# An FFN output product done as a two-by-two block product with seven block matmuls

## The chip, the cores and the metric

The kernel runs on one core of one Trainium2 chip. The metric is the device time of one launch in microseconds; the time before is the median of three runs. A profiled execution of the same program gives the trace that the rows below come from.

## The reference, cut to what matters

One encoder layer on 1024 tokens of width 1024. It begins and ends with a half-step feed-forward network (FFN) of 2816 features, and the change concerns both of these:

```
def _swiglu(x, w_in, w_out):
    gate, up = jnp.split(x @ w_in, 2, axis=-1)
    return (jax.nn.silu(gate) * up) @ w_out

x = x + 0.5 * _swiglu(_rmsnorm(x, n1_g), ffn1_w_in, ffn1_w_out)
...                                # projections, two attention mixers, merge
x = x + 0.5 * _swiglu(_rmsnorm(x, n3_g), ffn2_w_in, ffn2_w_out)
return _rmsnorm(x, nf_g)
```

With g = silu(gate) * up, the product that is changed is g @ w_out: 1024 tokens by 2816 features by 1024 outputs.

## The kernel before

**Number format.** Every operand of a large product is split by `split` (L81) into two fp32r numbers: ScalarE (ACT) casts it to `hi` (L82), VectorE (DVE) subtracts to get `lo` (L83). A product is then three matmuls, hi by hi, hi by lo and lo by hi.

**First half of an FFN, `ffn_in` (L321).** It walks the 22 feature tiles (128 features each). The product with `w_in` is already a two-by-two block product with seven block matmuls per tile: seven weight operands are made by `ffn_weights` (L297, additions on GpSimd, called POOL, at L309; splits on ACT and DVE), and the seven token operands are fixed (`operands`, L228: four of them live in the big buffers `bigA` and `bigB`, three in a pool `ex`). `product` (L335) issues 12 matmuls of 128x512 per operand into three PSUM banks, some of which it continues after a copy was taken (the copies are L354, L357, L360, L363). The result g of a tile is split, and stored to a DRAM buffer `g_d` as `goh`/`gol` halves (two stores of 512 KB for a tile); the last two tiles are kept in SBUF.

**Second half, `ffn` (L381).** x (4 MB) is loaded once and stays in SBUF. `out_rows` (L215) takes two feature tiles at a time: for each of 8 token tiles and 2 output halves it issues 6 matmuls of 128x512 (`mm3`, L118) into one of three PSUM banks tagged `S`, and DVE adds the bank to x (L226). The two tiles kept come first, then pairs whose g halves are loaded from `g_d` (four loads of 512 KB, contiguous 4 KB per partition) and whose weights (`weights`, L88) come from `w_out` as two rows blocks of 512 KB, split in 1024-wide instructions. The last tiles (two in the first FFN, four in the second) are handed back as a function and run interleaved with the norm that follows. In the second FFN, two of these last tiles lie in a buffer `spare` in `bigA`.

**Order.** The program is written in the order above, but a list scheduler orders the instructions of each engine before the run: an instruction written earlier goes first among those that are ready in its own timing model, and loads go out as soon as their buffer is free there. All DMAs go through one queue on SyncE (SP). On the chip every engine takes its list strictly in order.

```
# L215, the loop of out_rows
for t in tiles:
    for n in range(2):
        po = self.bank("S")
        ...
        self.mm3(po, [...])                    # 6 matmuls for a pair of feature tiles
        nc.vector.scalar_tensor_tensor(xs, po, scale, xs, ALU.mult, ALU.add)
```

Of the kernel before, what the change touches and what calls it, by code (L numbers as in the profile page):

```python
# [19 lines left out]
P = 128  # L20
SEQ = 1024
# [18 lines left out]
FILL_LATER = 250  # L40
EDGE = 280


class Layer:
# [276 lines left out]
    def ffn_in(self, w_in, ops, ph, g_d, first, ws):  # L321
# [16 lines left out]
        for i in range(NF):  # L338
# [7 lines left out]
            gh, gl = (ph.tile([P, SEQ], F32R, tag="t4", name=self.uid("g"), bufs=self.t4) for _ in range(2))  # L346
            for c in range(0, 512, m):
                cols = slice(c, c + m)
                w = iter(ws)
                bx, by, bz = (self.bank(t)[:, :m] for t in ("mm", "tp", "S"))  # L350
                e1, e2, e3, e5 = (ph.tile([P, 512], F32, tag="t2", name=self.uid("e"), bufs=8)[:, :m]
                                  for _ in range(4))
                product(bx, next(w), ops["b11"], cols, True)
                nc.scalar.copy(e1, bx)  # L354
                product(by, next(w), ops["b21"], cols, True)
                product(bx, next(w), ops["t2"], cols, False)
                nc.scalar.copy(e2, bx)  # L357
                nc.vector.tensor_tensor(e1, by, e1, ALU.add)
                product(bz, next(w), ops["t1"], cols, True)
                nc.scalar.copy(e5, bz)  # L360
                nc.scalar.activation(e1, e1, AF.Silu)
                product(bx, next(w), ops["t3"], cols, False)
                nc.scalar.copy(e3, bx)  # L363
                nc.gpsimd.tensor_tensor(e3, e3, e5, ALU.add)
                product(bz, next(w), ops["b22"], cols, False)
                nc.vector.tensor_tensor(e2, bz, e2, ALU.add)
                nc.scalar.activation(e2, e2, AF.Silu)
                nc.vector.tensor_tensor(e2, e2, e3, ALU.mult)
                product(bx, next(w), ops["t4"], cols, False)
                nc.vector.tensor_tensor(e1, bx, e1, ALU.mult)  # L370
                for n, e in ((1, e2), (0, e1)):
                    tok = slice(n * 512 + c, n * 512 + c + m)
                    self.split(gh[:, tok], gl[:, tok], e)
            if i < NF - 2:
                self.dma(g_d[i, 0], gh)
                self.dma(g_d[i, 1], gl)
            else:
                kept.append((gh, gl))
        return kept

    def ffn(self, x_d, w_in, w_out, g_d, ex, es_ex, first, ws=None, big=False):  # L381


        ph, es_ph = self.open("ph", bufs=1)
        ops = ex if first is None else self.operands(ex)
        self.t4 = 4 if first is None else 6
        kept = self.ffn_in(w_in, ops, ph, g_d, first, ws)
# [6 lines left out]
        def load(pool, f):  # L394
            out = []
            for i in (f, f + 1):
                g = [pool.tile([P, SEQ], F32R, tag=t, name=self.uid(t), bufs=2) for t in ("goh", "gol")]
                for j in range(2):
                    self.dma(g[j], g_d[i, j])
                out.append(tuple(g))  # L400
            return out
# [4 lines left out]
        self.w_eng = self.nc.vector  # L406
        self.out_rows(x, kept, weights(NF - 2), 0.5, range(NT))
        es_ph.close()
        go, es_go = self.open("go", bufs=1)
        end = 4 if big else 2  # L410
        for n, f in enumerate(range(0, NF - 4, 2)):
            cur = load((xo, go)[n % 2], f), weights(f)
            if f < NF - 2 - end:
                self.out_rows(x, *cur, 0.5, range(NT))
        f = NF - 4
        if big:
            spare = self.hp.tile([P, 8, SEQ], F32R, tag="bigA", name=self.uid("spare"))
            g, w = [(spare[:, 2 * j], spare[:, 2 * j + 1]) for j in range(2)], []
            for j in range(2):
                for h in range(2):  # L420
                    self.dma(g[j][h], g_d[f + j, h])
                raw = self.raw()
                self.dma(raw, w_out[(f + j) * P:(f + j + 1) * P, :])
                w.append((spare[:, 4 + 2 * j], spare[:, 5 + 2 * j]))
                self.split(*w[j], raw)
            cur = cur[0] + g, cur[1] + w
        else:
            cur = load(go, f), weights(f)

        def close():  # L430
            es_go.close()
            es_xo.close()

        return x, lambda tiles: self.out_rows(x, *cur, 0.5, tiles), close
# [494 lines left out]
    def run(self):  # L929
# [11 lines left out]
        g_d = [self.dr.tile([NF - 2, 2, P, SEQ], F32R, name=f"g_d{j}") for j in range(2)]  # L941
# [4 lines left out]
        def first(ops, ph):  # L946
            xs = {}

            def load(ts):
                for t in ts:  # L950
                    xs[t] = ph.tile([P, D], F32, tag="t4", name=self.uid("x0"), bufs=6)
                    self.dma(xs[t], x_d[t])
# [20 lines left out]
        x, rows, close = self.ffn(x_d, io["ffn1_w_in"], io["ffn1_w_out"], g_d[0], ex, es_ex, first)  # L973
# [94 lines left out]
        x, rows, close = self.ffn(x2_d, io["ffn2_w_in"], io["ffn2_w_out"], g_d[1], ops2, es_ex, None, ws, True)  # L1068
# [56 lines left out]
```

## Time and profile before

| | us |
|---|---|
| median of 3 runs | 2391.39 (2390.85 to 2392.74) |
| profiled execution, its own time | 2389.99 |
| span of its trace | 2388.2 |
| mean granted TensorE clock | 0.978 |

The span runs from the first to the last instruction of the trace; the execution's own time has 1.8 us more around it. PE is TensorE's matmuls, PEld its weight loads, DVE VectorE, ACT ScalarE, POOL GpSimd, SP the queue that issues all DMAs. Matmul ends in the trace are modelled: successive matmuls overlap, so the distance between starts, not the duration, is what one costs.

### The profile page before, as it was taken

The numbers are of one execution on the slowest core, as the hardware profiler recorded it, in microseconds if no ns is written. First come the engines' busy times: TensorE is split into PE (matmuls) and PEld (weight loads), VectorE is DVE, ScalarE is ACT, GpSimd is POOL, SyncE is SP. The second block draws the span as 40 slices with busy tenths as digits, with TensorE's granted clock in tenths as the row PEclk, the third lists the DMA queues.
The fourth block names the chain that finished last, engine by engine and source line by source line (L and its number), as shares of the span: only waits on it lengthen the run. The fifth ranks groups of instructions, "written<-read, shape, count | busy, mean of one in ns | idle before, by whom it ended". The sixth has DMA issues, their size and how long they took to land. (4 is left out here: it accounts for less than half of the span.)

```text
span 2388.2 us, 30574 instructions
## 1 busy us (share of the span) xinstructions
PE 2265.6 (95%) x10928; PEld 1893.1 (79%) x10928; DVE 1517.9 (64%) x2917; ACT 1010.3 (42%) x1971; POOL 589.8 (25%) x492
## 2 busy tenths in 40 slices
PE   4999999999998999899998999999799999999998
PEld 3877777778887988687778888878688888878886
DVE  7555555456657459798895378677655555546565
ACT  5444444410104454667743377633444444431012
POOL 6433333100005000223220043221733343300000
PEclk7999999999999999899999999999799999999999
DMA  4233333354414023455523241373233333354331
GB/s 134 89 106 106 106 106 106 106 203 159 159 71 146 1 80 98 131 127 136 126 71 103 87 159 49 112 250 110 89 106 115 106 106 106 106 218 169 132 142 71
DMA packets 204217, 280.82 MB, mean 118 GB/s; under 512 B 12064, under 2 KB 150304, under 8 KB 203552
## 3 DMA queue, kind: packets, MB, share of 16 engines
q1 hardware_dynamic: 204064, 278.86, 35.9%
q8 instruction: 86, 1.41, 0.3%
q14 instruction: 67, 0.55, 0.1%
HBM read 186.55 MB, written 79.69 MB: 111 GB/s over the span
## 5 line engine op out<-in xcount | busy, mean ns | idle before, releaser
L226 DVE SCALAR_TENSOR_TENSOR x<-S,x 128x512 f32<-128x512 f32 x400 | 270.6, 689 | 201.6 <-PE S L118 200.8
L83 DVE TENSOR_TENSOR wop<-raw,wop 128x512 fp32r<-128x512 f32 x210 | 150.3, 723 | 204.5 <-ACT wop L82 203.9
L82 ACT CAST whi<-raw 128x1024 fp32r<-128x1024 f32 (+1 forms) x90 | 85.6, 974 | 413.9 <-PE S L118 335.8
L335 PE MATMUL mm<-bigA,wop 128*128 128x512 f32 (+1 forms) x736 | 236.4, 384 | 10.6 <-ACT e L357 10.6
L335 PE MATMUL S<-bigA,wop 128*128 128x512 f32 (+1 forms) x736 | 235.1, 382 | 5.3 <-POOL wop L83 4.1
L118 PE MATMUL S<-wlo,goh 128*128 128x512 f32 x608 | 236.8, 389 | 0.0
L118 PE MATMUL S<-whi,gol 128*128 128x512 f32 x608 | 236.7, 389 | 0.0
L118 PE MATMUL S<-whi,goh 128*128 128x512 f32 x608 | 232.9, 393 | 1.9 <-DVE bigB L83 1.5
L82 ACT CAST wop<-raw 128x512 fp32r<-128x512 f32 x224 | 137.4, 625 | 103.7 <-PE mm L335 44.9
L335 PEld LDWEIGHTS mm<-bigA,wop 128*128 128x128 f32 x736 | 136.6, 188 | 46.0 <-ACT e L357 19.8
L118 PE MATMUL mm<-bigA,whi 128*128 128x512 f32 x384 | 156.0, 406 | 16.0 <-ACT whi L82 10.0
L83 DVE TENSOR_TENSOR wop<-s,wop 128x512 fp32r<-128x512 f32 x84 | 91.5, 1090 | 115.7 <-ACT wop L82 115.4
L335 PEld LDWEIGHTS S<-bigA,wop 128*128 128x128 f32 x736 | 137.6, 190 | 32.7 <-POOL wop L83 4.5
L118 PE MATMUL mm<-bigA,wlo 128*128 128x512 f32 x384 | 155.2, 405 | 2.1 <-POOL wlo L83 2.1
L118 PE MATMUL mm<-bigB,whi 128*128 128x512 f32 x384 | 154.9, 403 | 0.2 <-DVE bigB L83 0.2
L643 POOL TENSOR_SCALAR p<-p,z 128x640 f32<-128x640 f32 (+7 forms) x128 | 92.5, 726 | 211.8 <-DVE z L642 143.9
L83 POOL TENSOR_TENSOR wlo<-raw,whi 128x1024 fp32r<-128x1024 f32 (+1 forms) x32 | 67.7, 2114 | 301.1 <-ACT whi L82 292.3
L335 PE MATMUL S<-bigB,wop 128*128 128x512 f32 (+1 forms) x368 | 140.4, 382 | 0.1
L335 PE MATMUL mm<-bigB,wop 128*128 128x512 f32 (+1 forms) x368 | 139.8, 380 | 0.0
L118 PEld LDWEIGHTS S<-whi,goh 128*128 128x128 f32 x608 | 114.1, 188 | 31.5 <-DVE x L226 6.3
L309 POOL TENSOR_TENSOR raw<-raw,s 128x512 f32<-128x512 f32 x42 | 54.6, 1300 | 332.4 <-DVE wop L83 332.4
L335 PE MATMUL mm<-b,wop 128*128 128x512 f32 (+1 forms) x552 | 134.5, 381 | 0.0
(257 smaller groups left out, 5375.4 us busy)
## 6 DMA issues: line engine op xcount, KB each, us to landing
raw<-in_ffn_w_in_dram SPq DMA_DIRECT2D x88, 512.0 KB, 4.1
g_d<-g SPq DMA_DIRECT2D x80, 512.0 KB, 5.0
raw<-in_ffn_w_out_dram SPq DMA_DIRECT2D x44, 512.0 KB, 6.9
goh<-g_d SPq DMA_DIRECT2D x38, 512.0 KB, 5.2
gol<-g_d SPq DMA_DIRECT2D x38, 512.0 KB, 6.1
raw<-in_w_in_dram SPq DMA_DIRECT2D x28, 512.0 KB, 5.4
x<-in_x_dram SPq DMA_DIRECT2D x16, 512.0 KB, 7.5
x_d<-x SPq DMA_DIRECT2D x16, 512.0 KB, 2.6
```

What stands on the lines that cost most here:

```text
L82: self.nc.scalar.copy(hi, src)
L83: (eng or self.nc.vector).tensor_tensor(lo, src, hi.bitcast(F32), ALU.subtract)
L118: nc.tensor.matmul(out, lhsT=a, rhs=b, start=(i == 0), stop=(i == len(steps) - 1))
L226: nc.vector.scalar_tensor_tensor(xs, po, scale, xs, ALU.mult, ALU.add)
L309: nc.gpsimd.tensor_tensor(out, x, y, op)
L335: nc.tensor.matmul(out, lhsT=l, rhs=r, start=start and j == 0, stop=j == len(steps) - 1, skip_group_check=True)
L643: nc.gpsimd.tensor_scalar(p, p, z, 1.0, ALU.mult, ALU.mult)
```

## The change

For 16 of the 22 feature tiles (`NS = 16`), the output product is done in eight pairs of tiles. For a pair, the token rows p and p+4 and the two feature tiles make a two-by-two block matrix of g, the two feature tiles and the two output halves one of w_out, and the block product is formed from seven block products in place of eight.

- In `ffn_in`, the seven g operands of a pair are made as soon as both tiles of g are there: four 128x512 additions on POOL, seven splits, and seven stores of 512 KB to a new DRAM buffer `gs_d` (before: four splits and four stores of 512 KB for a pair). One operand is made after the even tile, six after the odd one. The temporary tag `t2` gets 10 buffers in place of 8; the tag `t4` has 4 buffers in both FFNs (before 6 in the first). Two of the first x tiles use the tag `s`.
- In `ffn`, `weight_ops` makes the seven weight operands of a pair: four 128x512 subtractions on POOL and seven 512-wide splits, into one of three 32 KB slots (`bigA`, `bigB`, and one in the pool `go`).
- `load_parts` loads the operands of a pair for one token pair p: 14 runs of 512 B per partition, 896 KB. Two pairs are worked at a time; the operands of the next p are loaded into the other of two pools while the current block runs.
- `block_rows` issues 42 matmuls for two pairs and one p: seven block products of 6 matmuls into three banks. Bank bx takes products 0, 2, 4 and 6, each continuing the sum in it; bz takes 3 and 5; by takes 1. After each product DVE adds the bank to a part of x, and the next product into this bank follows that addition.
- The four remaining streamed tiles (16 to 19) are loaded into the third slot as eight loads of 512 KB (`rest`); the two tiles kept are done first, as before, with `out_rows`.

```diff
+NS = 16
 def ffn_in(...)
-            if i < NF - 2:
-                self.dma(g_d[i, 0], gh)
-                self.dma(g_d[i, 1], gl)
...
+            def part(q, j, src):
+                t = ph.tile([P, SEQ], F32R, tag="t4", bufs=4).rearrange("p (h c) -> p h c", h=2)
+                self.split(t[:, 0], t[:, 1], src)
+                self.dma(gs_d[q, :, 2 * j:2 * j + 2, :], t)
...
+            elif i % 2 == 0:
+                a11, a21 = e1, e2
+                part(q, 0, a11)
             else:
+                a12, a22 = e1, e2
+                s1 = ph.tile([P, 512], F32, tag="t2", bufs=10)
+                nc.gpsimd.tensor_tensor(s1, a21, a22, ALU.add)
+                part(q, 1, a12)
+                nc.gpsimd.tensor_tensor(a21, a11, a21, ALU.subtract)
+                part(q, 6, a22)
+                nc.gpsimd.tensor_tensor(a11, s1, a11, ALU.subtract)
+                part(q, 3, s1)
+                nc.gpsimd.tensor_tensor(a12, a12, a11, ALU.subtract)
+                part(q, 4, a21)
+                part(q, 2, a11)
+                part(q, 5, a12)
 def ffn(...)
+        slots = [self.hp.tile([P, 8, 2, 512], F32R, tag=t) for t in ("bigA", "bigB")]
+        def weight_ops(q):
+            ra, rb, rs = self.raw(), self.raw(), self.raw()
+            for r, f in ((ra, 2 * q), (rb, 2 * q + 1)):
+                self.dma(r, w_out[f * P:(f + 1) * P, :])
+            b11, b12, b21, b22, t3, t2 = (r[:, c:c + h] for r in (ra, rb, rs) for c in (0, h))
+            sub(t3, b22, b12)
+            sub(b12, b12, b11)
+            sub(t2, b22, b12)
+            dst = slots[q % 3]
+            for j, src in enumerate((b11, b21, t2, b12, t3, b22, b21)):
+                self.split(dst[:, j, 0], dst[:, j, 1], src, self.w_eng)
+                if j == 1:
+                    sub(b21, b21, t2)
+            return dst
+        def load_parts(q, p):
+            t = pools[p % 2].tile([P, 7, 2, P], F32R, tag="gs", bufs=2)
+            self.dma(t.rearrange("p o h c -> p (o h) c"), gs_d[q, :, :, p * P:(p + 1) * P])
+            return t
+        def block_rows(ws, gs, p):
+            bx, by, bz = (self.bank(t) for t in ("mm", "tp", "S"))
+            done = {0: ((p, 0),), 1: ((p, 0),), 2: ((p, 1),), 3: ((p + 4, 1),),
+                    4: ((p + 4, 1),), 5: ((p, 1),), 6: ((p + 4, 0),)}
+            for j, bank in enumerate((bx, by, bx, bz, bx, bz, bx)):
+                ...                       # 6 matmuls, start only for j in (0, 1, 3)
+                for t, n in done[j]:
+                    add(t, n, bank)
+        for c in range(0, NS // 2, 2):
+            nxt = []
+            for p in range(4):
+                ahead = None
+                if p < 3:
+                    ahead = [load_parts(c + k, p + 1) for k in range(2)]
+                elif c + 2 < NS // 2:
+                    ahead = [load_parts(c + 2 + k, 0) for k in range(2)]
+                if p == 0 and c + 2 < NS // 2:
+                    nxt.append(weight_ops(c + 2))
+                block_rows(ws, gs, p)
+                gs = ahead
+            if nxt:
+                nxt.append(weight_ops(c + 3))
+                ws = nxt
+        rest = slots[2]...                # the third slot, seen as 4 tiles x 2 halves x 1024
+        for f in range(4):
+            for j in range(2):
+                self.dma(rest[:, f, j], g_d[f, j])
```

## Rows read from the trace of the kernel before

**Rows 1.** The page: busy time by engine, and TensorE's granted clock in 40 slices.

```profile
PE 2265.6 (95%) x10928; PEld 1893.1 (79%) x10928; DVE 1517.9 (64%) x2917; ACT 1010.3 (42%) x1971; POOL 589.8 (25%) x492
PEclk7999999999999999899999999999799999999999
```

**Rows 2.** The chain of waits near its start: start us, us, what.

```profile
2141.52 0.70 DVE x L226
2142.22 0.04 issue
2142.27 234.40 PE S L118 x1026
```

**Rows 3.** Busy time by stretch, with granted clock, DMA share and GB/s.

```profile
2142.00:2376.00 234.00, 233.73 (x1024) 191.67 (x1025) 140.68 (x219) 29.39 (x39) 0.00 (x0) 1.00 0.37 138
500.00:732.00 232.00, 229.83 (x1009) 187.50 (x1008) 140.38 (x212) 27.90 (x37) 10.50 (x6) 1.00 0.36 135
2127.00:2142.00 15.00, 13.25 (x56) 9.96 (x54) 7.68 (x9) 6.38 (x9) 1.30 (x1) 1.00 0.98 383
1695.00:1705.00 10.00, 5.45 (x22) 4.79 (x23) 6.18 (x6) 2.38 (x5) 10.00 (x8) 0.50 0.00 1
```

**Rows 4.** Groups by line and operation: xcount, busy us, mean ns, idle before.

```profile
L226 DVE SCALAR_TENSOR_TENSOR x<-S,x 128x512 f32<-128x512 f32 x400 | 270.6, 689 | 201.6 <-PE S L118 200.8 <-DMA sgm<-bra_d 0.7
L82 ACT CAST wop<-raw 128x512 fp32r<-128x512 f32 x224 | 137.4, 625 | 103.7 <-PE mm L335 44.9 <-PE S L335 33.1 <-PE tp L335 11.7
L309 POOL TENSOR_TENSOR s<-raw 128x512 f32<-128x512 f32 x42 | 54.7, 1304 | 27.8 <-DVE wop L83 22.6 <-DMA raw<-in_ffn_w_in_dram 5.2
L309 POOL TENSOR_TENSOR raw<-raw,raw 128x512 f32<-128x512 f32 x48 | 80.4, 1677 | 0.0
```

**Rows 5.** The timeline of DVE where one pair of tiles follows another.

```profile
2160.30 0.69 DVE L226 SCALAR_TENSOR_TENSOR x<-S,x 128x512 f32<-128x512 f32 x1 [0.67 <-PE S L118]
2160.90 2.35 DVE L83 TENSOR_TENSOR wlo<-raw,whi 128x1024 fp32r<-128x1024 f32 x2
2163.47 1.89 DVE L226 SCALAR_TENSOR_TENSOR x<-S,x 128x512 f32<-128x512 f32 x3 [0.21 <-PE S L118]
```

**Rows 6.** The timeline of POOL and DVE in the first half of the second FFN.

```profile
1870.36 1.29 POOL L364 TENSOR_TENSOR e<-e,e 128x512 f32<-128x512 f32 x1 [6.00 <-ACT e L363]
1872.27 1.30 POOL L309 TENSOR_TENSOR s<-raw 128x512 f32<-128x512 f32 x1 [0.62 <-DVE wop L83]
...
1870.83 1.36 DVE L83 TENSOR_TENSOR wop<-s,wop 128x512 fp32r<-128x512 f32 x1 [2.47 <-ACT wop L82]
1872.41 0.69 DVE L366 TENSOR_TENSOR e<-S,e 128x512 f32<-128x512 f32 x1 [0.22 <-PE S L335]
```

**Rows 7.** Write regions: first product of the first FFN, a later write into its operand.

```profile
36.92 0.58 PE L335 MATMUL S<-bigA,wop 128*128 128x256 f32 x1
59.78 0.58 ACT L82 CAST bigA<-tp 128x512 fp32r<-128x512 f32 x1
```

**Rows 8.** The timeline of SP's queue around the start of the second FFN's output.

```profile
2139.54 4.11 SPq L79 DMA_DIRECT2D spare<-g_d  x4
2144.66 0.33 SPq L79 DMA_DIRECT2D raw<-in_ffn_w_out_dram  x1
2160.33 0.32 SPq L79 DMA_DIRECT2D goh<-g_d  x1
```

**Rows 9.** DMA from 1886.2 to 1890 us: one w_in load, 512 B runs, alone.

```profile
DMA packets 1041, 0.54 MB, mean 142 GB/s; under 512 B 16, under 2 KB 1040, under 8 KB 1040
q1 hardware_dynamic: 1040, 0.52, 47.1%
DMA to landing us min/median/max: 3.6/3.6/3.6
```

**Rows 10.** DMA from 600 to 660 us: loads with 4 KB runs alone.

```profile
q1 hardware_dynamic: 2592, 9.44, 42.1%
```

**Rows 11.** The w_in loads of 1850 to 1960 us, stores of g beside them.

```profile
DMA to landing us min/median/max: 3.6/4.7/5.3
```

**Rows 12.** Waits of PE in the first half of each FFN (80 to 480, 1740 to 2130 us): total us, times, longest.

```profile
PE mm L335 <- ACT e L357: 8.5, 19, 0.5
PE mm L335 <- ACT e L354: 0.8, 1, 0.8
...
PE mm L335 <- ACT e L357: 1.4, 2, 0.7
```

**Rows 13.** Waits of PE from 1685 to 1714 us.

```profile
PE S L335 <- POOL wop L83: 4.1, 1, 4.1
```

More of the change, by code (lines that the diff above doesn't have):

```diff
@@ L319, in ffn_weights, with feature, ffn_in @@
             yield w
-    def ffn_in(self, w_in, ops, ph, g_d, first, ws):
+    def feature(self, w, ops, cols, product, e1, e2, e3, e5):
+        nc = self.nc
+        m = e1.shape[1]
+        bx, by, bz = (self.bank(t)[:, :m] for t in ("mm", "tp", "S"))
+        product(bx, next(w), ops["b11"], cols, True)
+        nc.scalar.copy(e1, bx)
+        product(by, next(w), ops["b21"], cols, True)
+        product(bx, next(w), ops["t2"], cols, False)
+        nc.scalar.copy(e2, bx)
+        nc.vector.tensor_tensor(e1, by, e1, ALU.add)
+        product(bz, next(w), ops["t1"], cols, True)
+        nc.scalar.copy(e5, bz)
+        nc.scalar.activation(e1, e1, AF.Silu)
+        product(bx, next(w), ops["t3"], cols, False)
+        nc.scalar.copy(e3, bx)
+        nc.gpsimd.tensor_tensor(e3, e3, e5, ALU.add)
+        product(bz, next(w), ops["b22"], cols, False)
+        nc.vector.tensor_tensor(e2, bz, e2, ALU.add)
+        nc.scalar.activation(e2, e2, AF.Silu)
+        nc.vector.tensor_tensor(e2, e2, e3, ALU.mult)
+        product(bx, next(w), ops["t4"], cols, False)
+        nc.vector.tensor_tensor(e1, bx, e1, ALU.mult)
+    def ffn_in(self, w_in, ops, ph, g_d, gs_d, first, ws):
         nc = self.nc
@@ L345, in ffn_in @@
                 ws = first(ops, ph)
-            gh, gl = (ph.tile([P, SEQ], F32R, tag="t4", name=self.uid("g"), bufs=self.t4) for _ in range(2))
+            e1, e2, e3, e5 = (ph.tile([P, 512], F32, tag="t2", name=self.uid("e"), bufs=10) for _ in range(4))
             for c in range(0, 512, m):
[L348 to L370, printed above, removed]
@@ L392, in ffn @@
             self.dma(x[:, t, :], x_d[t])
[L394 to L401, printed above, removed]
+        self.w_eng = nc.vector
+        slots = [self.hp.tile([P, 8, 2, 512], F32R, tag=t, name=self.uid("slot")) for t in ("bigA", "bigB")]
@@ L403, in weights @@
         def weights(f):
             return [self.weights((w_out[i * P:(i + 1) * P, :], D)) for i in (f, f + 1)]
-        self.w_eng = self.nc.vector
-        self.out_rows(x, kept, weights(NF - 2), 0.5, range(NT))
+        w = weights(NF - 2)
+        ws = [weight_ops(q) for q in (0, 1)]
+        gs = [load_parts(q, 0) for q in (0, 1)]
+        self.out_rows(x, kept, w, 0.5, range(NT))
         es_ph.close()
         go, es_go = self.open("go", bufs=1)
[L410 to L414, printed above, removed]
@@ L415, in ffn @@
-        f = NF - 4
-        if big:
[L417 to L421, printed above, removed]
+        slots.append(go.tile([P, 8, 2, 512], F32R, tag="slot", name=self.uid("slot")))
+        gsp, es_gsp = self.open("gsp", bufs=1)
+        pools.append(gsp)
+        for c in range(0, NS // 2, 2):
[13 more added lines that the diff above has]
+                ws = nxt
@@ L423, in ffn @@
                 self.dma(raw, w_out[(f + j) * P:(f + j + 1) * P, :])
[L424 removed]
+                w.append(tuple(last.tile([P, D], F32R, tag=f"w{j}{k}", name=self.uid("w")) for k in range(2))
+                         if j == 3 else tuple(self.wp.tile([P, D], F32R, tag=k, name=self.uid(k), bufs=3)
+                                              for k in ("whi", "wlo")))
                 self.split(*w[j], raw)
[L426 removed]
@@ L427, in ffn @@
         else:
-            cur = load(go, f), weights(f)
+            es_last = None
+            self.out_rows(x, g[:2], weights(f), 0.5, range(NT))
+            g, w = g[2:], weights(f + 2)
         def close():
+            if es_last is not None:
+                es_last.close()
             es_go.close()
             es_xo.close()
-        return x, lambda tiles: self.out_rows(x, *cur, 0.5, tiles), close
+        return x, lambda tiles: self.out_rows(x, g, w, 0.5, tiles), close
     def rope(self, y, t, nh, pool):
```

55 lines of the change are left out of this document (46 added, 9 removed).

## The prediction, on record before the changed kernel ran

> **What bounds the kernel now.** I read the page first: TensorE works in 95% of the span and no other engine in more than 64% [rows 1]. Then the chain of waits: from 2142.27 us to the end of the second FFN's output it is one piece, 1026 matmuls in 234.40 us, with no wait of note in it [rows 2]. That is 0.2285 us for one matmul of 128x512, the unit of all that follows. Third the stretches: in both output stages PE is busy all the time at a granted clock of 1.00, VectorE for 60% and the DMA engines for 0.36 to 0.37 [rows 3]. So a matmul less here is time less, as long as VectorE, the loads and the weights keep up. The question is how much of the room beside PE the change uses up.
>
> **What it removes.** A pair of feature tiles costs 2 x 8 x 2 x 3 = 96 matmuls now and 4 x 7 x 3 = 84 afterwards. Eight pairs and two FFNs: 192 matmuls less, 192 x 0.2285 = 43.9 us. The rest of the sum is what is lost of this. A block of `block_rows` is 42 matmuls, 9.60 us, and there are 16 in an FFN; one of its seven products is 1.37 us.
>
> **Load of the token operands (d).** A block needs two loads of 896 KB, 3584 runs of 512 B, while the block before it runs, since their buffers come free when the block before that ends. The nearest row is a load of w_in with the same run length, alone on the queue: 1040 packets at 47.1% of 16 engines over 3.8 us, 27.5 ns for each packet, and 3.6 us from issue to landing, so 1.8 us of fixed delay around 1.8 us of data [rows 9]. Two loads: 3584 x 27.5 / 16 = 6.2 us of data + 1.8 + 0.3 for the issue = 8.3 us, against 9.60: hidden, with 1.3 us to spare. Weights for the next pairs share the queue. A 512 KB load with 4 KB runs takes 128 x 175 / 16 = 1.4 us (2592 packets, 42.1% of 60 us, [rows 10]); two that stand ahead of the token loads cost 2.8 - 1.3 = 1.5 us. I take one such meeting per FFN, 3 us; below nothing if they fall into the gaps, and above, if the landing scales whole with the packets from the median of 4.7 us that loads beside stores show [rows 11], 4.7 x 3.5 = 16.4 us a block, 6.8 us too many 30 times.
>
> The Trainium skill's page "DMA: Bandwidth & Descriptors" (Specifications) gives 512 B as the size from which a transfer runs at line rate. By that the two loads would take 1.835 MB at the 383 GB/s that long runs reach [rows 3], 4.8 us, and d would be nothing. The trace does not bear it out: 512 B in 27.5 ns is 18.6 GB/s an engine, 4 KB in 175 ns is 23.4.
>
> **VectorE and the weights in the blocks (a).** Additions hardly change in number (7 in place of 8 for the same 48 matmuls' work), 0.69 us each [rows 4]. Splits do: seven of 512 columns for a pair in place of two of 1024 (1.18 us each, [rows 5]). In four blocks, 38.4 us, VectorE has 28 x 0.69 = 19.3 us of additions and 14 x 0.69 = 9.7 us of splits. ACT (14 x 0.625 = 8.8 us) and POOL (8 subtractions of 1.3 to 1.7, at most 13.4 us) stay well below 38.4 [rows 4], so they cost nothing while PE covers them.
>
> What is new is that an addition now holds PE up sooner. Before, three banks let it be late: at 2160.90 two splits of 2.35 us went ahead, three additions piled up behind them, and the stage did not stop [rows 5]. Now product 2 writes into the bank that the addition after product 0 reads, with 1.37 us between. The modelled end lies 0.16 us behind the slot, the addition takes 0.70 and PE follows about 0.05 after [rows 2], so it may be late by 0.4 us, and by one product more where PE's list puts an independent product (3, in another bank) ahead. Splits come first again, being written earlier. First block: the third slot opens when the kept tiles are done, and seven splits are ready together, 4.8 us; 4.8 - 0.4 - 1.4 = 3.0 us lost. At the two later places where a slot opens, subtractions on POOL spread the splits; I take a third of it, 1 us each. The other slot is refilled piece by piece during the block that uses it last: buffers are tracked by region, since PE read one half of a `bigA` operand at 36.92 us and ACT still wrote the other at 59.78 [rows 7]. That costs nothing that I can see. Sum 5 us an FFN, **a = 10**. Bounds: 2 us if the lists interleave well, 36 if VectorE itself limits (a rival).
>
> **Passing from the first half to the second (b).** The first two pairs' splits, 14 x 0.69 = 9.7 us, fall on the two kept tiles (96 matmuls, 21.9 us, with 16 x 0.69 = 11.0 us of additions): 20.7 of 21.9 us. Nine splits can come in one go, 6.2 us, while three banks hold 4.1. I take 1.5 us an FFN, **b = 3**; from 0 to 12.
>
> **The four remaining tiles (c).** Their eight loads go into the third slot, whose last reader is the third group's last block, and a load leaves as soon as its buffer is free: four loads into `spare` left at 2139.54, 180 us ahead of their use [rows 8]. So six or eight of them, 8.2 to 10.9 us at 1.4 each, stand before the next token loads. These are then late: data from 15.7 us (7.5, where the load before ends, + 8.2), landing near 22.4 where 19.2 is wanted, a loss of 3.2 us; 5.9 with all eight in front, 8.7 with two weights as well. I take 5 us an FFN, **c = 10**, from 4 to 17. Waits up to 0.8 us left the clock at 1.00 in these stages [rows 3, 12]. After waits of up to 4.1 us it was at 0.50, the lower of its levels, 1.2 of 2.4 GHz, in the stretch of 1695 to 1705 [rows 3, 13]. Such a stretch could add 5 us (10 us of matmuls at half the rate) to each of two stalls; I take none and keep 10 for the range.
>
> **The first half (e).** It gets three splits and three stores more for a pair, and four operations on POOL. In the 38 us of a pair that is 3 x 0.69 on VectorE, 3 x 0.625 on ACT, 4 x 1.3 to 1.7 on POOL [rows 4] and 3 x 1.4 us of DMA [rows 10]: all behind PE. On SP a store that waits for its split holds up the w_in loads behind it, which are wanted a tile later, 19 us. The copies out of PSUM on ACT are not all hidden: in the first FFN PE waits for them 19 times, 8.5 us, in the second only twice, 1.4 us [rows 12], in the same code. More work on ACT, unevenly placed (one operand after an even tile, six after an odd one), can bring this order into the second FFN (+8.5), and a new order can lose it in the first (-8.5). I take half of the first, **e = 4**, from -8 to 17. Without the cover, all casts and splits of the part show: 3 x (0.69 + 0.625) x 8 = 32 us an FFN. The moved x tiles and the buffer counts I cost at nothing: the loads still leave in the same order, and `t4` had 4 buffers in the second FFN already.
>
> **Sum.** -43.9 + 10 + 3 + 10 + 3 + 4 = -13.9 us. Against the profiled execution, 2390.0 (span 2388.2 and 1.8 around it), that is 2376.1; the median of the runs is 1.4 above it: **2377.5 us**. Changes under 0.2%, 4.8 us, can't be told from none.
>
> **Rivals.**
>
> *Loads longer than a block (slower).* Place: each of 30 blocks; price: 30 x (load - 9.60). Without d, 16.9 us of gain are left, and 21.7 must be lost to count as slower, so it decides from 0.72 us over, a load of 10.3 us. For it: loads beside stores landed in 4.7 us, up to 5.3 [rows 11], and runs 2 KB apart have no row here. Against: no store to DRAM runs in this stage, and the load that was alone fits. At 10.8 us: 2391.4 - 43.9 + 27 + 36 = 2410.5. Chance 0.16.
>
> *VectorE becomes the bound (slower).* A split beside a POOL operation took 1.36 us in place of 0.69, while an addition from PSUM kept 0.69 [rows 6]. If POOL's subtractions meet all splits, four blocks have 28 x 0.69 + 14 x 1.36 = 38.4 us on VectorE, as much as PE, and with additions in tight loops neither runs freely. At 6 us for each of six such groups a is 36: 2391.4 - 43.9 + 20 + 36 = 2403.5. Against: POOL is busy for 13.4 of the 38.4 us at most. Chance 0.10. The Trainium skill's page "SBUF — State Buffer" (SBUF: two separate sides) has the rule: VectorE with two SBUF inputs and a GpSimd operation that reads SBUF lock each other out for the whole instruction. By that rule it would go this way; the two durations agree with it.
>
> *Everything hides.* a to e at their low ends, 2 + 0 + 4 + 0 + 0: 2353.5 to 2364. For it: PE was busy through every pair's splits before [rows 3, 5]. Chance 0.22.
>
> *Used up.* Losses of 39 to 48 us, each term half again as large and one stall at the lower clock: 2386.6 to 2396.2, about 2391. Chance 0.14.
>
> **How the numbers follow.** The forecast, 2364 to 2386.6 with 2377.5 in it, has 0.38. Faster: 0.38 + 0.22 = 0.60; same 0.14; slower 0.16 + 0.10 = 0.26. The range goes from the everything-hidden end, 2353, to a load of 10.8 us, 2410; beyond lie mainly half of that rival and a little of the first half's upper bound. The likeliest case's own range is 2364 to 2387.
>
> **What would show it.** Right: 192 matmuls fewer; in the output stages PE waits for VectorE after split bursts by up to 3 us, and for `gs` loads only once an FFN, by 3 to 9 us, after the `rest` loads; landing of `gs` near 5 us for the first and 8 for the second of a block. Wrong: a wait for `gs` in most blocks (first rival), VectorE over 90% there with splits of 1.36 us (second), or an output stage that is shorter by 22 us an FFN without waits (third). The copies' waits in the first half, line 357's old place, show e. What would make it wrong most of all is the token load, whose price is taken from a load with another stride.

## The result, and the profile after

The changed kernel takes 2434.7 us (median of 4 runs, 2426.5 to 2437.1) against 2392.1 for the kernel before on the same chip: ratio 1.0174, interval 1.0155 to 1.0192. It is 43 us slower; the forecast was 2377.5, and the time lies outside its range. The profiled execution took 2426.5 us (span 2424.7), 8 us less than the median; the stage lengths below come from it.

Two lines of the page of the changed kernel, to be read beside [rows 1]:

```profile
PE 2240.1 (92%) x10736; PEld 1852.1 (76%) x10736; DVE 1595.7 (66%) x3009; ACT 1064.7 (44%) x2095; POOL 784.1 (32%) x620
PEclk9999999999999999899999999999899999999999
```

The 192 matmuls are gone (10928 to 10736) and the clock is no lower, but PE is busy for 92% in place of 95%: the time went into waits. The waits of PE over the whole span (waiting group, releaser: total us, times, longest), changed kernel:

```profile
PE mm L361 <- ACT e L331: 24.3, 38, 1.2
PE mm L468 <- DMA gs<-gs_d: 23.1, 22, 2.3
...
PE mm L468 <- DVE x L455: 11.6, 11, 1.9
...
PE S L119 <- ACT g L83: 6.3, 2, 3.1
...
PE S L468 <- DVE x L455: 2.6, 2, 1.3
...
PE mm L468 <- POOL raw L436: 1.6, 1, 1.6
```

The first line belongs to the first halves: line 331 is the copy that was line 357, and its waits were 8.5 and 1.4 us [rows 12]. The others are the output stages, where the kernel before ran almost without waits [rows 2, 3]. `gs` are the token operands, line 468 is the matmul of a block, and line 455 the addition that follows a product. The busy times of a stretch within the first of them, 510 to 690 us, in the changed kernel, columns as in [rows 3] (length; PE, PEld, DVE, ACT, POOL; clock, DMA share, GB/s):

```profile
510.00:690.00 180.00, 161.42 (x684) 126.03 (x682) 120.45 (x166) 30.33 (x48) 40.81 (x27) 1.00 0.73 214
```

PE stands for 18.6 of 180 us at a granted clock of 1.00; VectorE is busy for 67%, far from a bound on average, and the DMA share has doubled from the 0.36 of [rows 3].

Stage lengths, worked out from the traces: a first half runs from the first to the last matmul with a `wop` operand, an output stage from there to the first `mm<-bigA` matmul of the projections (the stage between the two FFNs begins with them), or to the end of the span. "Without loss" is the kernel before less 96 x 0.2285 = 21.9 us in each output stage.

| us | first half 1 | output 1 | between | first half 2 | output 2 |
|---|---|---|---|---|---|
| before | 455.8 | 256.5 | 946.2 | 442.1 | 250.7 |
| without loss | 455.8 | 234.6 | 946.2 | 442.1 | 228.8 |
| after | 459.3 | 264.2 | 944.2 | 458.6 | 262.3 |

So the output stages lost 29.6 + 33.5 = 63.1 us where the terms a, b, c and d held 26, and the first halves 3.5 + 16.5 = 20.0 us where e held 4.

### The profile page after: what moved, and what is told of

The parts are those of the page before. It is cut to its first block, busy times and chain, and to the rows that moved or that the text cites. A ratio compares the mean times of both kernels' runs of the same rounds, so it can differ in the third digit from the quotient of the medians.

```text
span 2424.7 us, 30527 instructions
## 1 busy us (share of the span) xinstructions
PE 2240.1 (92%) x10736; PEld 1852.1 (76%) x10736; DVE 1595.7 (66%) x3009; ACT 1064.7 (44%) x2095; POOL 784.1 (32%) x620
## 4 chain that ended last, share of the span: by engine, by line
PE 39%; DVE 15%; DMA 7%; ACT 4%; issue 3%; POOL 1%; SPq 1%; ACTq 0%; DVEq 0%; POOLq 0%
PE mm L361 9%; PE S L119 7%; PE mm L119 6%; PE S L361 4%; DVE tkj L686 3%; DMA gs<-gs_d 3%; PE mm L468 2%; PE tp L361 2%; PE S L575 1%; PE pv L119 1%; DVE p L734 1%; PE S L576 1%; DVE ptl L84 1%; PE tp L760 1%; DMA raw<-in_w_in_dram 1%
## 5 line engine op out<-in xcount | busy, mean ns | idle before, releaser
L84 DVE TENSOR_TENSOR wop<-raw,wop 128x512 fp32r<-128x512 f32 x210 | 158.5, 763 | 159.1 <-ACT wop L83 158.6
L361 PE MATMUL mm<-bigA,wop 128*128 128x512 f32 (+1 forms) x736 | 238.5, 387 | 24.3 <-ACT e L331 24.3
L468 PE MATMUL mm<-slot,gs 128*128 128x512 f32 x768 | 201.0, 399 | 37.1 <-DMA gs<-gs_d 23.1
L468 PEld LDWEIGHTS mm<-slot,gs 128*128 128x128 f32 x768 | 141.5, 189 | 83.6 <-DMA gs<-gs_d 29.1
L119 PE MATMUL mm<-bigA,whi 128*128 128x512 f32 x384 | 155.5, 405 | 16.5 <-ACT whi L83 10.9
L83 ACT CAST slot<-raw 128x512 fp32r<-128x512 f32 x112 | 66.7, 620 | 228.5 <-PE mm L468 160.9
L455 DVE SCALAR_TENSOR_TENSOR x<-mm,x 128x512 f32<-128x512 f32 x128 | 87.6, 688 | 100.6 <-PE mm L468 100.2
L436 POOL TENSOR_TENSOR raw<-raw,raw 128x512 f32<-128x512 f32 x48 | 72.4, 1511 | 250.3 <-DVE slot L84 191.1
L84 DVE TENSOR_TENSOR g<-e,g 128x512 fp32r<-128x512 f32 x136 | 129.8, 982 | 16.9 <-ACT g L83 16.8
L84 DVE TENSOR_TENSOR wop<-s,wop 128x512 fp32r<-128x512 f32 x84 | 85.4, 1017 | 78.8 <-ACT wop L83 78.4
```

Source lines behind the costliest of these rows:

```text
L83: self.nc.scalar.copy(hi, src)
L84: (eng or self.nc.vector).tensor_tensor(lo, src, hi.bitcast(F32), ALU.subtract)
L119: nc.tensor.matmul(out, lhsT=a, rhs=b, start=(i == 0), stop=(i == len(steps) - 1))
L361: nc.tensor.matmul(out, lhsT=l, rhs=r, start=start and j == 0, stop=j == len(steps) - 1, skip_group_check=True)
L436: nc.gpsimd.tensor_tensor(out, x, y, ALU.subtract)
L455: nc.vector.scalar_tensor_tensor(xs, bank, 0.5, xs, ALU.mult, ALU.add)
```

## The experiments

All ratios are to the kernel before on the same chip, with 95% intervals; the changed kernel stands at 1.0174.

**Token loads left out.** Of the four blocks that share weights only the first loads its token operands, and the next three use them again, so this kernel leaves out 24 of the 32 loads of an FFN, and the rows of six of eight token tiles are computed from the first block's operands. (The pool that they lie in is changed to fit.)

```diff
-                    ahead = [load_parts(c + k, p + 1) for k in range(2)]
+                    ahead = gs
```

> Edit: operands are loaded for the first token pair of each group of four blocks only, and the other three blocks use them again; this leaves out 24 of the 32 loads of an FFN, and the rows of 6 of 8 token tiles are computed from the first pair's operands. Both theories on the loads: waits for gs vanish but for the group starts (under 5 us of 23.1), the time falls by 20 to 30 us. What is then left above 2391.4 - 43.9 = 2347.5 is VectorE's waits, the passing from the first half to the second, and the first half: by the waits of the trace some 14 + 8 + 20 = 42 us, so about 2390 profiled. If the time falls by less than 12 us, the loads were not what the output stage loses on.

2385.8 us, ratio 0.9975 [0.9964, 0.9987]: 49 us less than the changed kernel. The output stages are 240.1 and 234.5 us, 5.5 and 5.7 above "without loss". The same stretch as above in this kernel:

```profile
510.00:690.00 180.00, 178.63 (x785) 146.73 (x784) 128.39 (x182) 31.82 (x51) 43.39 (x28) 1.00 0.32 101
```

With the same splits, additions and subtractions PE is busy for 178.6 of 180 us, and its waits for additions fell from 14.2 us to 2.4 (1.2 + 1.2). So most of the loss of the output stages hangs on the token loads being there. This does not separate the loads from the order of the matmuls: without the loads the list scheduler makes another list for TensorE, in which two blocks run nearly side by side. The second of two begins 56 to 74 matmuls before the first ends (167 at the very first), and in the changed kernel 14 to 35 at nearly every place. That this list also gives the additions more room is argued here, not shown.

**Longer runs.** The layout in DRAM gives loads of one long run per partition (7 KB), and stores in 512 B runs:

```diff
-gs_d = tile([NS // 2, P, 14, 512])
+gs_d = tile([NS // 2, 4, P, 14, P])
...
-self.dma(gs_d[q, :, 2 * j:2 * j + 2, :], t)
+for h in range(2):
+    self.dma(gs_d[q, :, :, 2 * j + h, :]..., t[:, h]...)   # two half-size stores
```

> Edit: the operands lie in DRAM by token pair, so a load has 7 KB runs and the stores of the first half have 512 B runs; the order of work is the scheduler's as before. A load of a pair then takes some 2.4 us of data in place of 3.3 (896 KB at 383 GB/s), two of them 4.8 in place of 6.7. Theory B (the short runs make the load too long): waits for gs fall from 23.1 us under 5. Theory A (buffers held too long): the two buffer sets go round in 22 us for two blocks now, 15 us of holding and 7 of loading; 2 us less of loading still leave 10 us a block against 9.6, so waits fall to about 8 to 12 us. Either way the time falls by 10 to 25 us; stores with short runs cost 1.9 us in place of 1.4 each in a stage where the DMA engines are busy for 0.4, so nothing.

2441.7 us, 1.0207 [1.019, 1.0224]. In the output stages the waits for `gs` fell nearly as far as theory B said:

```profile
PE mm L470 <- DMA gs<-gs_d: 5.5, 8, 1.1
```

The output stages are 250.6 and 247.4 us, 28.5 shorter in all. Both theories missed the first halves, which are 476.0 and 476.8 us, 35 longer. The short runs only moved from the loads to the stores: ScalarE waited for a `t4` buffer that a store still read for 35.0 us in the first FFN (14.3 in the changed kernel, none before), and PE's waits for the copies of line 331 are 46.9 us in place of 24.3.

With hi and lo of an operand side by side, loads have 1 KB runs and stores keep 4 KB:

```diff
-t.rearrange("p (h c) -> p h c", h=2); gs_d = tile([NS // 2, P, 14, 512])
+t.rearrange("p (b h c) -> p b h c", b=4, h=2); gs_d = tile([NS // 2, P, 7, 4, 2, P])
```

> The token operands are laid out in DRAM with hi and lo of an operand side by side, so that a load has 896 runs of 1 KB in place of 1792 of 512 B; the stores keep 4 KB runs per partition. Theory A (each block lasts as long as its loads are late, by the price of short packets): a 1 KB packet lies between the 27.5 ns of 512 B and the 175 ns of 4 KB, about 49 ns, so a load's data takes 2.7 in place of 3.1 us; about half of what the 4 KB runs gave the output stages (29 us), and no loss in the first half: 2412 to 2424. The waits for gs fall from 23 us to about half. Rival (the bytes alone, or VectorE, set the block): within 3 us of 2434.7.

2427.9 us, 1.0151 [1.0138, 1.0165]: some 6 us better, the waits for `gs` 17.3 us in place of 23.1. The gain is about half of the least that theory A set: 1 KB runs help, but they leave most of these waits.

**The order of the blocks, and the bursts of splits.** The first kernel makes TensorE's list keep to the order written (each product behind the last matmul of the product before it):

```diff
+with self.tc.issue_after(self.last_block):
     for n, (l, r) in enumerate(steps):
         ins = nc.tensor.matmul(...)
+self.last_block = ins
```

> Edit: TensorE's matmuls of all blocks in the order written, product after product and block after block; nothing else changes. Theory A (held buffers): in the changed kernel the scheduler starts the next block before the current one is finished, so the operands of a block are held for some 15 us in place of 9.6 and the load for the block after next leaves some 6 us late. In order, a load has a whole block of time again: waits for gs fall from 23.1 us to under 6, waits for the additions on VectorE may grow by up to 10, the time falls by 10 to 20 us from 2434.7, to 2415 to 2425. Theory B (the pair of loads is longer than a block by itself, because of its 512 B runs): waits for gs stay above 20 us and the time does not fall by more than 5.

2431.6 us, 1.0166 [1.0142, 1.0191]. Half of theory A came true: waits for `gs` fell, if not quite under 6 us. The gain in time failed, since the waits for additions took their place. PE's waits in the blocks of this kernel:

```profile
PE mm L471 <- DVE x L455: 23.6, 13, 4.3
...
PE mm L471 <- DMA gs<-gs_d: 8.4, 6, 2.2
```

The timeline of VectorE in it (start, length, what) shows why: three splits of the next weights, one behind the other, take 4.74 us beside POOL's subtractions, ahead of three additions.

```profile
534.96 0.68 DVE L455 SCALAR_TENSOR_TENSOR x<-mm,x 128x512 f32<-128x512 f32 x1
535.57 4.74 DVE L84 TENSOR_TENSOR slot<-raw,slot 128x512 fp32r<-128x512 f32 x3
540.23 0.68 DVE L455 SCALAR_TENSOR_TENSOR x<-S,x 128x512 f32<-128x512 f32 x1
540.83 1.27 DVE L455 SCALAR_TENSOR_TENSOR x<-mm,x 128x512 f32<-128x512 f32 x2
```

The next kernel leaves the order to the scheduler and puts each split behind the addition of one product (the subtractions and loads a block earlier); the one after does both.

```diff
+                with self.tc.issue_after(self.last_add):
                     self.split(dst[:, j, 0], dst[:, j, 1], src, self.w_eng)
+                yield dst            # one turn after each product of a block
```

> The changed kernel with the splits spread alone, in the scheduler's own order of the blocks. Theory D (mixed halves of two blocks hold the token buffers longer than a block, so the loads stay late whatever VectorE does): waits for gs 20 us or more as before, 2425 to 2433. Rival (the splits are the whole loss of the output stages): waits for gs gone as well, 2413 to 2418.

> The changed kernel with the blocks in the order written and the splits spread one by one behind additions; loads of 512 B runs and first halves as in the changed kernel. Theory D (the price of the loads in the prediction was right, 8.3 us for two, and they fit into a block of 9.6 us as long as the blocks run one after the other): waits for gs stay near the 8 us of the order alone, waits for additions fall from 24 to about 10, 2413 to 2418. Rival (loads of 512 B don't fit even then): waits for gs 15 us or more, 2422 to 2431.

Spread alone: 2453.1 us, 1.0258 [1.0238, 1.0278], slower than either theory allowed. Both: 2408.0 us, 1.0075 [1.0063, 1.0087], some 24 us better than the changed kernel and better than theory D set; output stages 254.6 and 246.6. PE's waits in the blocks, first with the spread alone, then with both:

```profile
PE mm L473 <- DMA gs<-gs_d: 48.4, 34, 3.2
...
PE mm L473 <- DVE x L460: 1.6, 2, 0.8
```

```profile
PE mm L476 <- DVE x L460: 10.5, 14, 1.0
PE mm L476 <- DMA gs<-gs_d: 10.2, 6, 2.7
```

So the two faults cover each other: mend one alone and the other takes the time. TensorE's instruction list of the changed kernel, as the list scheduler made it, shows the first. One block in it (`mm_4227`, `gs_4121`/`4123`) and the next (`mm_4283`, `gs_4200`/`4202`):

```
L468 MATMUL mm_4283<-slot_3926,gs_4200 128x512 x3    next block, first pair
L468 MATMUL tp_4284<-slot_3926,gs_4200 128x512 x3
L468 MATMUL S_4285<-slot_3926,gs_4200 128x512 x3
L468 MATMUL mm_4227<-slot_3926,gs_4121 128x512 x3    last product of the block before
L468 MATMUL mm_4227<-slot_3730,gs_4123 128x512 x3
L468 MATMUL mm_4283<-slot_3730,gs_4202 128x512 x3    next block, second pair
```

The next block begins nine matmuls before the last product of this one. Call the matmuls between the last one that reads a buffer and the first one that reads its next content the cover of a load. Counted over the list, it is 18 to 33 matmuls for the first of the two loads of a block, the middle one 22.5: 22.5 x 0.2285 = 5.1 us. For the second load it is 27 to 47, the middle one 36, 8.2 us. With the spread alone the first has 21, 4.8 us. In the written order it is always 45 for both, 10.3 us. A load took, in the changed kernel and in the one with both (us from issue to landing, all loads together):

```profile
DMA to landing us min/median/max: 5.4/8.1/14.2
```

```profile
DMA to landing us min/median/max: 5.3/8.5/14.8
```

Taken apart in the trace of the changed kernel, the first load of a block landed 5.6 us after its issue in the median and the second 8.6, and a load left 0.03 us after its buffer came free. So 25 of 28 first loads (the 28 that go into a buffer which the same FFN used before) came later than their cover allows, by 0.9 us in the median and 2.9 at most, and 23 of 28 second ones. In the kernel with both the landings are 6.3 and 8.9 us, and none of the first loads and 8 of the second are late: the loads did not get faster, the cover grew. The kernel with 7 KB runs is the test from the other side. Its list has the cover of the changed kernel, its loads landed after 4.9 and 6.7 us, 12 and 4 of them were late, and the waits for `gs` nearly went. With 1 KB runs they landed after 5.5 and 8.1 us, and 21 and 15 were late. What counts is a load against its cover, and not against a block.

**Whose queue the weight rows use.**

```diff
-                self.dma(r, w_out[f * P:(f + 1) * P, :])
+                nc.scalar.dma_start(r, w_out[f * P:(f + 1) * P, :])
```

> Only this: the w_out rows from which the seven weight operands are made are loaded by ScalarE's queue in place of the one queue on SyncE. Theory B (the rows stand behind token loads that wait for their buffers, so the operands come late, VectorE's list stands still in front of them, and the additions behind it hold TensorE): PE's waits for VectorE in the blocks, 14 us in both FFNs, fall by half, and the token loads, no longer behind rows that wait for a buffer, leave earlier too: 2420 to 2428. Rival (what counts is how long the token operands stay in their buffers and how long they take; whose queue the rows use does not matter): within 3 us of 2434.7.

2456.5 us, 1.0265 [1.025, 1.0279]: theory B falls, and its rival, no change, missed as well. Waits for additions fell from 11.6 + 2.6 to 7.7 + 2.6 us, but those for `gs` rose from 23.1 to 36.2, although SP's queue now held hardly anything but token loads. Eight pairs of them, one behind the other:

```profile
542.27 88.14 SPq L80 DMA_DIRECT2D gs<-gs_d  x16
```

That is 11.0 us for a pair, but SP spends most of it waiting for buffers that TensorE still reads (104.8 us from 510 to 690 us): it is not the rows ahead of them in the queue that hold the loads up. The second load of a block landed after 9.2 us in the median, in place of 8.6; why the kernel became 22 us slower than the changed one stays open beyond that.

**The first half.** Product t1 is put behind t2 in TensorE's list, which gives the copy after the product in the same bank one product more:

```diff
+        with self.tc.issue_after(t2):
             product(bz, w1, ops["t1"], cols, True)
```

> Edit: in the first half of both FFNs, the product with t1 is issued behind the one with t2 on TensorE; nothing else changes. Theory: the scheduler's order (t1 before t2, so that t3 follows t2 directly and waits for the copy of the same bank) costs the 22.9 us of waits for line 331's copy in the two first halves. With the order forced they fall under 5 us and the time falls by 20 to 28 us, to 2407 to 2415. Rival: ACT has too much work for the copies to be in time in any order; then the same waits come back at another copy (line 328 or 337) and the time stays within 8 us of 2434.7.

2426.0 us, 1.0131 [1.0107, 1.0155], which misses the forecast. The waits for line 331 went, but 8.3 us came back at another copy (line 328), in part what the rival said. And feature tile 0 had used t1 as work while the operands were made: the first matmul of the first half started 18.6 us later (54.8 in place of 36.2 us), and the part between the FFNs was 27.6 us longer. From tile 1 on only:

> Product t1 is put behind t2 in TensorE's list for all feature tiles but the first, so that the copy after t2 has one product more of time; the first tile keeps its order. Theory A (the waits for the copies of line 331, 24.3 us in both FFNs, are what the first halves lost, and the earlier run of this order lost elsewhere only by its first tile): first halves 20 to 24 us shorter in all with the part between the FFNs unchanged: 2411 to 2416. Rival (the waits move to another bank or buffer): 2425 to 2435.

2420.7 us, 1.0125 [1.0112, 1.0138]: first halves 452.8 and 451.5 us, 13.6 less in all. Theory A holds in kind, with two thirds of its size; the 8.3 us of waits at line 328 are there as well, and the time missed its range. The other suspect was ScalarE, which stands at a cast until a store has left the `t4` buffer:

```diff
-t = ph.tile([P, SEQ], F32R, tag="t4", bufs=4)
+t = ph.tile([P, SEQ], F32R, tag="t4", bufs=5)
```

> Five t4 buffers in place of four, nothing else. Theory A (ScalarE, in order, stands at a cast whose t4 buffer a store still reads, 14.3 us in four waits in the first FFN, and the PSUM copies behind it come late): these waits fall to about nothing, PE's waits for the copies of line 331 fall by a third or more, time down by 5 to 10 us: 2424 to 2430. Rival (the copies are late because of the mere amount and order of work on ScalarE): waits for line 331 near 11.5 us a half as before, time within 3 us of 2434.7.

2436.8 us, 1.0187 [1.0169, 1.0205]: no gain. ScalarE's wait in the first FFN, from 60 to 490 us, in the changed kernel and with five buffers:

```profile
ACT g L83 <- DMA gs_d<-g: 14.3, 4, 3.7
```

```profile
ACT g L83 <- DMA gs_d<-g: 22.8, 8, 3.3
```

One buffer more took no wait away, so this run can't clear or convict the wait.

**All together.** 1 KB runs, five buffers and t1 behind t2; then, besides, the blocks in order; then the spread splits as well; then the weight rows on ScalarE's queue:

> 1 KB runs, five t4 buffers and t1 behind t2 from the second tile on, together. Theory A: the gains add up, output stages 14 us and first halves 24 us shorter: about 2397. Rival (a common limit under them, VectorE's list): 2410 to 2420.

> The kernel with 1 KB runs, five t4 buffers and t1 behind t2 (2403.9) and, besides, the blocks in the order written on TensorE. Theory A (in the scheduler's order the halves of two blocks are mixed and hold their token buffers for longer than a block; with shorter loads the written order lets every load hide): waits for gs below 3 us in an FFN, 2390 to 2398. Rival (with the order forced, late additions on VectorE take the place, as in the run with the order alone): waits for line 455's additions 20 us or more in both FFNs, 2400 to 2406.

> As the kernel before it in this set, and the seven splits of a pair's weight operands are put into VectorE's list one by one, each behind the addition of one product of a block (subtractions and loads a block earlier). Theory C (bursts of splits in front of additions are the prediction's term a, some 4 us each time): waits for the additions fall from some 20 us to under 8 in both FFNs, 12 us faster than the same kernel without it: 2380 to 2390. Rival (the additions are late because of their own operands or the banks): no gain beyond 3 us.

> As the kernel before it, with the w_out rows on ScalarE's queue. Theory B: the token loads leave as soon as their buffers are free, another 3 to 8 us: 2375 to 2385. Rival: same as the kernel before it within 3 us.

| | us | ratio | first halves | output 1, 2 |
|---|---|---|---|---|
| three together | 2403.9 | 1.0055 [1.0041, 1.0069] | 446.6, 444.0 | 263.8, 257.5 |
| and in order | 2396.0 | 1.0014 [1.0005, 1.0022] | 447.3, 446.4 | 258.1, 253.6 |
| and splits spread | 2381.0 | 0.9952 [0.994, 0.9963] | 446.2, 446.4 | 251.1, 246.6 |
| and rows on ScalarE | 2383.5 | 0.9968 [0.9955, 0.9981] | 447.2, 447.2 | 252.6, 248.7 |

The first fell between its theory and the rival. The second is where its theory A put it, with the 21.9 us of waits for additions that the rival named. The splits in turn give 15 us once the order is right (the time of theory C, though 11.2 us of waits for additions are left where it had under 8), in place of a loss of some 20 without it. Whose queue the rows use makes no gain here either. The third kernel is 0.5% faster than the kernel before. Its output stages are still 16.5 and 17.8 us above "without loss": order, spread and 1 KB runs took away 29 of the 63 us, while the kernel without loads has 11.2 left. PE's waits for additions and for `gs` in its blocks, 11.2 + 6.4 us, are about half of what is left; the rest is not put down to a cause here. What this third kernel still loses in a block with seven splits is seen in VectorE's timeline:

```profile
529.64 0.67 DVE L84 TENSOR_TENSOR slot<-raw,slot 128x512 fp32r<-128x512 f32 x1
530.24 0.68 DVE L463 SCALAR_TENSOR_TENSOR x<-mm,x 128x512 f32<-128x512 f32 x1
530.84 1.40 DVE L84 TENSOR_TENSOR slot<-raw,slot 128x512 fp32r<-128x512 f32 x1
532.16 0.68 DVE L463 SCALAR_TENSOR_TENSOR x<-S,x 128x512 f32<-128x512 f32 x1
532.76 1.17 DVE L84 TENSOR_TENSOR slot<-raw,slot 128x512 fp32r<-128x512 f32 x1
533.85 0.68 DVE L463 SCALAR_TENSOR_TENSOR x<-mm,x 128x512 f32<-128x512 f32 x1
534.45 1.18 DVE L84 TENSOR_TENSOR slot<-raw,slot 128x512 fp32r<-128x512 f32 x1
535.56 0.68 DVE L463 SCALAR_TENSOR_TENSOR x<-mm,x 128x512 f32<-128x512 f32 x1
```

VectorE has no idle time there, and PE waits for the last of them:

```profile
536.29 1.66 PE L479 MATMUL mm<-slot,gs 128*128 128x512 f32 x6 [0.76 <-DVE x L463]
```

POOL's timeline in it has a subtraction of 1.30 us from 530.39, of 1.61 from 531.77 and of 1.63 from 533.46: the splits of 1.40, 1.17 and 1.18 us stand beside these, the one of 0.67 stands alone. Spread over two blocks for every other set:

> The fastest kernel so far (2381.0), with the first of each two sets of seven splits spread over two blocks in place of one. In a block with seven splits VectorE had no idle time and TensorE waited 0.9 to 1.0 us for the last addition, in the blocks between none. Theory (VectorE is the bound of just these blocks): six such waits go, 5 to 6 us faster: 2374 to 2377. Rival (the wait comes from the order in which the additions stand): no change.

2378.8 us, 0.9952 [0.9936, 0.9968]: no measurable gain. Fewer but longer waits took the place of the short ones (8 in place of 15): for additions they are 11.1 us as before (10.6 + 0.6), with one of 3.1, so the theory falls.

**The kernel before with the first half's order alone.**

> The kernel before with only t1 put behind t2 from the second tile on: what the first half's order is worth without the change, so that the mended kernel is compared fairly. PE's waits for the copies were 8.5 and 1.4 us there: 3 to 9 us faster, 2383 to 2389, if they go; no change if the order only moves them.

2375.6 us, 0.994 [0.9928, 0.9952], first halves 442.3 and 442.0 us. It is as fast as the mended kernels or a little faster. Against it, the block product in its best form here shows no gain.

## Why the prediction was wrong

**The 192 matmuls at 0.2285 us.** Right in number, and the price holds: without the loads each output stage came within 6 us of it.

**Load of the token operands (d).** This is the step that failed, at the sentence that two loads run "while the block before it runs, since their buffers come free when the block before that ends". The price was 1 us low, which alone would not have hurt: 8.3 us were predicted for two loads, and from the issue of the first to the landing of the second they took 9.3 us in the median of the changed kernel, still under a block's 9.60. That the landing of a single load has a median of 8.1 us, so near to 8.3, is chance. The packets were a little dearer than assumed. From 540 to 600 us, the changed kernel moved

```profile
DMA packets 20917, 12.91 MB, mean 215 GB/s; under 512 B 259, under 2 KB 20274, under 8 KB 20914
q1 hardware_dynamic: 20914, 12.87, 76.3%
```

The trace records each packet: the 20015 of 512 B took 30.3 ns in the mean, against 27.5 in the prediction, and 640 of 4 KB took 194 ns. (The prediction's 175 ns for 4 KB does not come out of [rows 10] as they stand: 288 of the 2592 packets are of 4 bytes, and the other 2304 took 174 ns.) The Trainium skill's page "DMA: Bandwidth & Descriptors" (Specifications), by which 512 B runs at line rate, is not borne out here either: in the kernel with three changes 1 KB packets took 51.6 ns in the same stretch, 19.8 GB/s an engine against 16.9. What was wrong is the cover. The prediction took the written order for TensorE's order; but a list scheduler makes that, and in its list 5.1 us lie between the last read of the first buffer of a block and the first read of its next content, and 8.2 for the second, where the prediction had 9.60 for the two loads together. The term d held 3 us, and PE's waits for `gs` in the blocks were 23.1. In SP's timeline of the changed kernel four pairs of loads take from 539.36 to 582.98 us, 10.9 us a block in place of 9.60:

```profile
539.36 23.65 SPq L80 DMA_DIRECT2D gs<-gs_d  x6
...
573.56 1.55 SPq L80 DMA_DIRECT2D gs<-gs_d  x2
576.22 2.96 SPq L80 DMA_DIRECT2D raw<-in_ffn_w_out_dram  x2
582.98 22.13 SPq L80 DMA_DIRECT2D gs<-gs_d  x6
```

**VectorE in the blocks (a).** The mechanism was right, a burst of splits ahead of additions. That 4.74 us were measured where 4.8 was estimated is luck: these are three splits of 1.58 us beside POOL's subtractions, where the estimate had seven of 0.69 and took the subtractions for a help. The size was hidden by the late loads: 23.6 us of waits once the order was mended, and 15 us gained by spreading, where a had 10. The sentence that an addition may be late by one product more where the list "puts an independent product (3, in another bank) ahead" named the mixing, but saw only its good side: it is what makes room for the additions, and it takes that room from the loads.

**The four remaining tiles (c).** Six `rest` loads do stand before the token loads, as predicted, but around them PE waits for `gs` for 3.2 us from 625 to 700 us in the changed kernel and 0.7 us from 600 to 712 in the third of the kernels all together (called the mended one below), where c had 5 an FFN.

**From the first to the second half (b).** 1.5 us an FFN were predicted, from VectorE. In the mended kernel PE waits there 3.1 us for a cast of the kept g on ScalarE (1.0 before) and 2.4 to 3.1 us for the first token loads, about 5 more than before in each FFN, by another mechanism.

**The first half (e).** Mis-sized: 20.0 us, where 4 was taken and the bound was 17. That the unfavourable order of the copies could come into the second FFN was foreseen; it did (1.4 to 10.9 us of waits), and the first FFN, taken as already bad, got worse (8.5 to 11.5 in the stretch of [rows 12]). t1 behind t2 takes 13.6 of the 20 us away. With 1 KB runs and five buffers as well, 13.7 more go, though each of these alone gave the first halves nothing; why they work only together stays open.

**The rivals.** "Loads longer than a block" had the right direction and the right wait, with the wrong reason: two loads, 9.3 us, are not longer than a block; the time for them is shorter. Its 2410.5 had the first half at 4 us. "VectorE becomes the bound" is false for the changed kernel (67% busy), and half true for single blocks of the mended one, where it is never idle and splits beside POOL take twice as long (1.40 us in place of 0.67; 1.58 in the burst). The Trainium skill's page "SBUF — State Buffer" (SBUF: two separate sides) has VectorE with two SBUF inputs and a GpSimd operation that reads SBUF lock each other out for the whole instruction. These durations agree with it: the three splits that met a subtraction ended 0.55 us after it did. Additions that read PSUM kept 0.68 us.

## What to carry to other kernels

A double buffer covers a load only for the time between the last read of a buffer and the first read of its next content, in the list that the engine really runs: count it there, in instructions, before pricing the load against the work of a block. Where two faults hide each other, a run that mends one alone shows no gain or a loss, so try the pair before dropping either. And try a mended version's side gains on the old kernel as well: here a change of order in the first half was worth as much there as all the rest.

## What was not expected of the hardware

Packets of 1 KB took 51.6 ns and those of 512 B 30.3 ns in the same stretch of two kernels, so twice the length cost 1.7 times the time. Stores in 512 B runs, two of half the size in place of one, made the first halves 35 us longer, though DMA stood at a share of 0.48 there (0.43 in the changed kernel, 100 to 450 us). Taking the weight rows off the queue that carries the token loads did not bring these any earlier: their median landing is 8.1 us in both kernels.
